# S5 parameters moved to the first feed-forward stage, and a prologue that builds its operand from PSUM, in a three-mixer decoder trunk

## The chip, the cores and the metric

The kernel runs on one core of one Trainium2 chip. The metric is device time of one execution, in microseconds (us); lower is better. Engines are named as the profile names them: PE is TensorE (PEld its weight loads), DVE is VectorE, ACT is ScalarE, POOL is GpSimd, and SP is SyncE, which issues most DMAs here.

## What is computed

A two-layer decoder trunk on 512 tokens of width 1024, all in float32. Each layer adds half a SwiGLU, a mixer (Mamba-2 SSD in layer 0, S5 in layer 1), and half a second SwiGLU; a final normalisation ends it.

```python
def rmsnorm(x, g):
    return x * lax.rsqrt(jnp.mean(x * x, axis=-1, keepdims=True) + NORM_EPS) * g

def swiglu(h, w_in, w_out):
    gate, up = jnp.split(h @ w_in, 2, axis=-1)
    return (jax.nn.silu(gate) * up) @ w_out

for i in range(DEPTH):                       # 2 layers
    x = x + 0.5 * swiglu(rmsnorm(x, ffn1_norm[i]), ffn1_w_in[i], ffn1_w_out[i])
    h = rmsnorm(x, mix_norm[i])
    x = x + (ssd_mixer(h, ...) if i == 0 else s5_mixer(h, ...))
    x = x + 0.5 * swiglu(rmsnorm(x, ffn2_norm[i]), ffn2_w_in[i], ffn2_w_out[i])
return rmsnorm(x, final_norm)
```

The S5 mixer needs operators that depend only on parameters (64 groups of 64 complex states: `lam`, `log_step`, B, C and a skip term `d`). The kernel builds them beside the matmuls of earlier stages and keeps them in DRAM as `d_H`, `d_P` and the phase tables `d_t`.

## The kernel before

Activations are kept transposed, `xT[d]`: eight tiles of 128 channels x 512 tokens. Every projection is split exactly into a high and a low part: `split_w` casts a weight tile `wst` (128 x 1024, 512 KB) on ACT to `whi` and subtracts on DVE to get `wlo`; `proj` then does 24 matmuls per tile (8 blocks x hi·H, hi·L, lo·H). `wst` has four buffers, `whi` and `wlo` three each, and the accumulators `mm` four PSUM banks. So the load of tile n waits until tile n-4 is split, and the cast of tile n waits until PE is done with tile n-3. Below, tile 0, 1, 2, ... are the weight tiles of a feed-forward stage in order: gate and up of f=0, gate and up of f=1, and so on.

Stages run in the order f1_0, ssd, f2_0, f1_1, s5, f2_1. A stage can start its matmuls before the token norm is known, since 1/rms (`rbc`) is applied when the accumulators are read (`gt`, `up`). Four tiles fit into the four banks; the fifth needs `gt` of the first, and so needs `rbc`: squares are summed by `compact_sum` on PE, a Newton iteration of small DVE operations gives `nw_y`, PE broadcasts it (`bcast_rows`), and ACT copies it to `rbc`.

`ffn` calls one closure of its list `fill` after each f and each output tile. Closures of `s5_setup` are handed to f1_0 (part 0: parameters of lambda, powers, tables) and to f2_0 (part 1: it loads back the powers PR, PI, ER, EI, loads B and C in eight pieces with `load_bc`, fills the zero half of `d_P` with `load_d`, and builds the operators with `ops` and `ops_pe`). The order on each engine's queue is set by the build's list scheduler, which also moves instructions of closures ahead of or behind those of the stage; each engine then runs its queue strictly in order. In the prologue x arrives in four DMAs of 512 KB, is transposed on PE in 32 blocks, copied to `xT` on DVE, and made into the operands `hH` and `hL` from `xT`.

Of the kernel before, what the change touches and what calls it, by code (L numbers as in the profile page):

```python
# [1113 lines left out]
```

## Time and profile before

| | |
|---|---|
| median of 3 runs | 2125.33 us (2125.13 to 2127.54) |
| span of the profiled execution | 2124.6 us |
| PE busy | 2055.0 us, 97% of the span |
| DVE, ACT, POOL busy | 1256.6, 793.7, 44.9 us |
| bytes by DMA | 228.50 MB |

The span is the time from the first to the last instruction of one execution; no other time of that execution is recorded, and it lies 0.7 us below the median of the runs. PE carries almost the whole span, so what matters is where PE stands still and at which clock it runs. "Idle" in a row is the time an engine's queue waited just before an instruction, and what is named behind the arrow is what released it.

### The profile page before, as it was taken

How to read it: one execution, taken by the hardware profiler on the slowest of the kernel's cores; microseconds unless marked ns; L12 is line 12 of the kernel's file. 1: busy time of each engine (PE TensorE's matmuls, PEld its weight loads, DVE VectorE, ACT ScalarE, POOL GpSimd, SP SyncE). 2: the span in 40 equal slices, each digit the busy share in tenths (PEclk: the TensorE clock that was granted, in tenths of full speed). 3: DMA queues.
4: the chain of work that ended last, by engine and by line, in shares of the span. 5: the costliest groups of instructions: out<-in, count | busy, mean ns of one | idle time of the engine just before them, and what ended most of it. 6: DMA issues, size and time to landing. Idle time of an engine off the chain costs nothing.

```text
span 2124.6 us, 27175 instructions
## 1 busy us (share of the span) xinstructions
PE 2055.0 (97%) x10755; PEld 1691.2 (80%) x10755; DVE 1256.6 (59%) x2171; ACT 793.7 (37%) x1146; POOL 44.9 (2%) x116
## 2 busy tenths in 40 slices
PE   6999999999999999699999999999996999999997
PEld 5888888888888887587788888888885788888886
DVE  6887445678875787477844454344457654434444
ACT  4223223566753664243422333232254433222222
POOL 1000000000000001000000000000001000000000
PEclk9999999999999999899999999999998999999999
DMA  5344333322223214756533363333357233332331
GB/s 153 110 130 138 91 99 83 99 74 76 70 72 91 77 41 117 123 148 174 154 95 100 94 201 92 99 96 99 95 159 244 83 100 89 99 100 81 108 92 58
DMA packets 408672, 228.50 MB, mean 108 GB/s; under 512 B 45656, under 2 KB 397072, under 8 KB 408544
## 3 DMA queue, kind: packets, MB, share of 16 engines
q1 hardware_dynamic: 383120, 200.24, 33.1%
q0 software_dynamic: 4272, 13.66, 2.8%
q10 hardware_dynamic: 21152, 12.86, 2.1%
q8 instruction: 84, 1.38, 0.3%
q14 instruction: 44, 0.36, 0.1%
HBM read 204.64 MB, written 22.09 MB: 107 GB/s over the span
## 4 chain that ended last, share of the span: by engine, by line
PE 93%; DVE 3%; DMA 2%; ACT 1%; issue 1%; SPq 0%; POOL 0%; ACTq 0%; DVEq 0%
PE mm L203 29%; PE mm L205 29%; PE mm L204 29%; DMA p_B<-in_s_b_re_dram 1%; PE aux L464 1%; PE aux L414 0%; DVE z L919 0%; PE aux L457 0%; DMA wst<-in_ffn_w_in_dram 0%; PE aux L434 0%; DMA p_lrow<-in_s_lam_re_dram 0%; PE aux L135 0%; PE aux L204 0%; PE aux L205 0%; PE aux L203 0%
## 5 line engine op out<-in xcount | busy, mean ns | idle before, releaser
L194 ACT CAST whi<-wst 128x1024 fp32r<-128x1024 f32 (+2 forms) x357 | 361.1, 1013 | 953.6 <-PE mm L204 676.2
L203 PE MATMUL mm<-hH,whi 128*128 128x512 f32 x1800 | 706.4, 393 | 1.2 <-DVE gt L225 1.2
L205 PE MATMUL mm<-hH,wlo 128*128 128x512 f32 x1800 | 703.5, 391 | 0.0
L204 PE MATMUL mm<-hL,whi 128*128 128x512 f32 x1800 | 703.0, 391 | 0.0
L196 DVE TENSOR_TENSOR wlo<-wst,whi 128x1024 fp32r<-128x1024 f32 (+2 forms) x357 | 418.8, 1174 | 107.9 <-ACT whi L194 104.1
L203 PEld LDWEIGHTS mm<-hH,whi 128*128 128x128 f32 x1800 | 339.2, 189 | 73.1 <-issue 2.0
L205 PEld LDWEIGHTS mm<-hH,wlo 128*128 128x128 f32 x1800 | 338.8, 188 | 71.3 <-issue 0.4
L204 PEld LDWEIGHTS mm<-hL,whi 128*128 128x128 f32 x1800 | 339.1, 188 | 69.8
L204 PE MATMUL mm<-al,whi 128*128 128x512 f32 x704 | 275.8, 392 | 0.0
L205 PE MATMUL mm<-ah,wlo 128*128 128x512 f32 x704 | 275.3, 391 | 0.0
L203 PE MATMUL mm<-ah,whi 128*128 128x512 f32 x704 | 274.9, 391 | 0.0
L228 DVE TENSOR_TENSOR up<-mm,rbc 128x512 f32<-128x512 f32 x88 | 60.7, 690 | 222.2 <-PE mm L205 222.1
L240 DVE SCALAR_TENSOR_TENSOR xT<-mm,xT 128x512 f32<-128x512 f32 x96 | 66.1, 689 | 197.6 <-PE mm L205 197.6
L204 PEld LDWEIGHTS mm<-al,whi 128*128 128x128 f32 x704 | 132.1, 188 | 28.7 <-issue 0.2
L205 PEld LDWEIGHTS mm<-ah,wlo 128*128 128x128 f32 x704 | 132.1, 188 | 28.6 <-issue 0.2
L203 PEld LDWEIGHTS mm<-ah,whi 128*128 128x128 f32 x704 | 132.1, 188 | 28.3
L225 DVE TENSOR_TENSOR gt<-mm,rbc 128x512 f32<-128x512 f32 x88 | 60.7, 690 | 154.8 <-PE mm L205 149.4
L231 ACT CAST ah<-up 128x512 fp32r<-128x512 f32 x88 | 54.8, 623 | 66.3 <-DVE up L229 66.2
L340 DVE SCALAR_TENSOR_TENSOR cv<-raw,cols,cv 128x512 f32<-128x512 f32 x96 | 70.9, 745 | 0.7
L229 DVE TENSOR_TENSOR up<-up,gt 128x512 f32<-128x512 f32 x88 | 60.7, 690 | 7.8 <-ACT gt L226 0.7
L226 ACT ACTIVATE gt<-gt 128x512 f32<-128x512 f32 x88 | 55.1, 627 | 17.0 <-DMA d_P<-p_ks 13.2
L233 DVE TENSOR_TENSOR al<-up,ah 128x512 fp32r<-128x512 f32 x88 | 60.1, 684 | 1.4 <-ACT ah L231 1.4
(333 smaller groups left out, 1726.0 us busy)
## 6 DMA issues: line engine op xcount, KB each, us to landing
wst<-in_ffn_w_in_dram SPq DMA_DIRECT2D x176, 512.0 KB, 3.9
wst<-in_ffn_w_out_dram SPq DMA_DIRECT2D x64, 448.0 KB, 3.7
wst<-in_ssd_in_proj_dram SPq DMA_DIRECT2D x48, 512.0 KB, 4.0
wst<-in_ffn_w_out_dram SPq DMA_DIRECT2D x32, 512.0 KB, 4.2
opP<-d_P SPq DMA_DIRECT2D x16, 512.0 KB, 5.0
wst<-in_s_glu_w_dram POOLq DMA_DIRECT2D x12, 512.0 KB, 5.2
d_t<-p_cs POOLq DMA_DIRECT2D x8, 512.0 KB, 3.0
wst<-in_ssd_out_proj_dram SPq DMA_DIRECT2D x8, 512.0 KB, 4.1
```

The lines of the kernel that those rows point to most:

```text
L194: S.copy(hi, st)
L196: V.tensor_tensor(lo, st, hi.bitcast(F32), op=OP.subtract)
L203: PE.matmul(ps, hi[:, k], H[k], start=first and k == 0, stop=False)
L204: PE.matmul(ps, hi[:, k], L[k], start=False, stop=False)
L205: PE.matmul(ps, lo[:, k], H[k], start=False, stop=last and k == n - 1)
L225: V.tensor_tensor(gt, pg, pr.rbc, op=OP.mult)
L226: S.activation(gt, gt, AF.Silu)
L228: V.tensor_tensor(up, pu, pr.rbc, op=OP.mult)
L229: V.tensor_tensor(up, up, gt, op=OP.mult)
L233: V.tensor_tensor(al, up, ah.bitcast(F32), op=OP.subtract)
L240: V.scalar_tensor_tensor(xT[d], po, 0.5, xT[d], op0=OP.mult, op1=OP.add)
L340: V.scalar_tensor_tensor(cv, raw[:, 1 + j:T + 1 + j], col("cw", j * 32 + ct), cv, op0=OP.mult, op1=OP.add)
```

## The change

- B (`load_b`), C (`load_c`), the skip term and the zeros of `d_P` (`zeros`) are loaded or written in f1_0 instead of f2_0. C comes in three DMAs of 256 KB instead of 24 of 32 KB and is transposed there (`c_cols`); B comes in 16 DMAs instead of 32; the second stack of B is made from the first by a copy in SBUF (`swap_b`), and its sign goes into EI.
- The restacked B, B swapped and C are saved to DRAM and loaded back whole in f2_0 (`restore`).
- The zeros are issued from SP instead of POOL.
- The parameter pool of f1_0 no longer lies in the memory of the prologue's x. `tc.keep_in_program_order` (in `paced`, `expf` and others) forbids the scheduler to move that one instruction.
- x comes over SP's and ACT's queues; the first two weight tiles are fetched between its pieces; `hH` and `hL` are made from PSUM, and ACT and DVE run the prologue in written order. Squares come after all operands. The small masks and `cols` of other stages come later.

```diff
+    def paced(dst, src):
+        tc.keep_in_program_order(nc.sync.dma_start(dst, src))
...
-    for j in range(4):
+    def x_in(j, eng):
         js = slice(j * 256, j * 256 + 256)
-        nc.sync.dma_start(xt4[:, :, js], x[0].rearrange("(t p) d -> p t d", p=128)[:, :, js])
+        tc.keep_in_program_order(eng.dma_start(xt4[:, :, js], x[0].rearrange("(t p) d -> p t d", p=128)[:, :, js]))
+    x_in(0, nc.sync)
+    x_in(1, nc.scalar)
...
+    x_in(3, nc.scalar)
...
-            V.tensor_scalar(a, src, -87.0, 88.0, op0=OP.max, op1=OP.min)
+            tc.keep_in_program_order(V.tensor_scalar(a, src, -87.0, 88.0, op0=OP.max, op1=OP.min))
...
+        def load_b(i):
+            gs = slice(i * 8, i * 8 + 8)
+            for h, src in enumerate((s5_b_re, s5_b_im)):
+                paced(st["B1"][h * 64:h * 64 + 64, gs], src[0, gs].rearrange("g p c -> p g c"))
+        def swap_b():
+            for h in range(2):
+                paced(st["B2"][h * 64:h * 64 + 64], st["B1"][64 - h * 64:128 - h * 64])
+        def load_c():
+            st["crow"] = pp.tile([128, 8, 3, 64], F32, name="p_crow", bufs=1)
+            for j, src in enumerate((s5_c_re, s5_c_im, s5_c_re)):
+                paced(st["crow"][:, :, j], src[0].rearrange("(i a) c p -> (a c) i p", a=8))
...
+        def zeros():
             ov = d_P.rearrange("(c q) g m -> q c g m", q=8)
             for q in range(1, 8):
-                G.dma_start(ov[q, :, :, 128:128 + 16 * q], zz[:, None, 0:16 * q].to_broadcast([16, 64, 16 * q]))
+                paced(ov[q, :, :, 128:128 + 16 * q], zz[:, None, 0:16 * q].to_broadcast([16, 64, 16 * q]))
+        def c_cols(i):
+            p = aux_ps()
+            for k in range(2):
+                for j in range(2):
+                    PE.transpose(p[:, j * 256 + k * 128:j * 256 + k * 128 + 128],
+                                 st["crow"][:, 2 * i + k, j:j + 2].rearrange("g a b -> g (a b)"), ident)
+            S.copy(st["C"][:, :, 16 * i:16 * i + 16].rearrange("p a g c -> p a (g c)"),
+                   p.rearrange("p (a n) -> p a n", a=2))
...
+            V.tensor_scalar(EI.rearrange("p a b -> p (a b)"), EI.rearrange("p a b -> p (a b)"), st["sg"][:, 0:1], -1.0,
+                            op0=OP.mult, op1=OP.mult)
...
-            if i % 2 == 0:
-                load_bc(i // 2)
...
-        keep = ("PR", "PI", "ER", "EI")
+        keep = ("ER", "EI", "B1", "B2", "PR", "PI", "C")
         if part == 0:
+            first_loads()
             gen = lam()
-            return [load] + [lambda: next(gen)] * 6 + [save] + [lambda i=i: tables(i) for i in range(8)]
-        return [restore] + [f for i in range(8) for f in (
+            one = lambda: next(gen)
+            return ([both(load_c, masks), zeros, rows] + [one] * 6 + [lambda: save(("PR", "PI", "ER", "EI"))]
+                    + [both(lambda i=i: tables(i), lambda i=i: load_b(i)) for i in range(8)]
+                    + [lambda i=i: c_cols(i) for i in range(4)]
+                    + [lambda: save(("B1",)), swap_b, lambda: save(("C",)), lambda: None, lambda: save(("B2",))])
+        return [lambda: restore(keep[:2]), lambda: restore(keep[2:4]), lambda: restore(keep[4:6]), lambda: restore(keep[6:]),
+                lambda: None, lambda: None] + [f for i in range(8) for f in (
...
-    for d in range(KD):
-        p = aux_ps()
-        for t in range(4):
-            PE.transpose(p[:, t * 128:(t + 1) * 128], xt4[:, t, d * 128:(d + 1) * 128], ident)
-        V.tensor_copy(xT[d], p)
-        prep.take(d)
+    for j in range(2):
+        w0 = ffn1_w_in[0][:, j * FF:j * FF + 128]
+        st_, ins = fetch_w(w0, KD)
+        tc.keep_in_program_order(ins)
+        first.append(st_)
+        if j == 0:
+            x_in(2, nc.sync)
+    with tc.manual_schedule(engines={mybir.EngineType.Activation, mybir.EngineType.DVE}):
+        cols_of(3)
+        for d in range(KD):
+            p = (aux_ps, mm_ps)[d % 4 // 2]()
+            for t in range(4):
+                PE.transpose(p[:, t * 128:(t + 1) * 128], xt4[:, t, d * 128:(d + 1) * 128], ident)
+            g = col(prep.gain[0], prep.gain[1] + d)
+            S.activation(prep.H[d], p, AF.Copy, scale=g)
+            V.scalar_tensor_tensor(prep.L[d], p, g, prep.H[d].bitcast(F32), op0=OP.mult, op1=OP.subtract)
+            if d % 2:
+                S.copy(xT[d], p)
+            else:
+                V.tensor_copy(xT[d], p)
+            if d in (0, 4):
+                ready.append(split_w(first[d // 4], KD))
+        for d in range(KD):
+            prep.square(d)
```

What the engines then have in their queues differs at three places that the prediction uses. Rows of before carry before's line numbers, those of the change its own (L189 became L204, L203 to L205 became L222 to L224, L144 became L160, L594 and L614 became L53).

The first place is SP at the start of the program. Before, it holds x and then the weights of f1_0:

```order
L79 DMA xt_99<-in_x_dram 128x4x256 x4
L189 DMA wst<-in_ffn_w_in_dram 128x8x128 x16
L189 DMA wst<-in_ffn_w_out_dram 128x8x128 x8
L189 DMA wst<-in_ffn_w_in_dram 128x8x128 x14
L189 DMA wst<-in_ffn_w_out_dram 128x7x128 x8
```

Behind x there are only weights. In the change, the same queue from its start to C (`p_crow`); `p_zz` is the tile of zeros:

```order
L85 DMA xt_97<-in_x_dram 128x4x256
L204 DMA wst<-in_ffn_w_in_dram 128x8x128
L85 DMA xt_97<-in_x_dram 128x4x256
L204 DMA wst<-in_ffn_w_in_dram 128x8x128 x4
L53 DMA d_P<-p_zz 16x64x16
L53 DMA d_P<-p_zz 16x64x32
...
L53 DMA d_P<-p_zz 16x64x112
L204 DMA wst<-in_ffn_w_in_dram 128x8x128 x5
L53 DMA p_crow<-in_s_c_re_dram 128x8x64
L53 DMA p_crow<-in_s_c_im_dram 128x8x64
L53 DMA p_crow<-in_s_c_re_dram 128x8x64
```

Seven writes of zeros now stand between weight tiles 4 and 5, and C stands behind tile 9.

The second place is PE in f1_0, where four tiles are done and the norm is broadcast. Before:

```order
L204 MATMUL mm<-hL,whi 128x512
L205 MATMUL mm<-hH,wlo 128x512
L144 MATMUL aux<-ident,nw_y 128x128 x4
L573 MATMUL aux<-ident,p_lrow 128x64 x2
L203 MATMUL mm<-hH,whi 128x512
```

In the change:

```order
L223 MATMUL mm<-hL,whi 128x512
L224 MATMUL mm<-hH,wlo 128x512
L160 MATMUL aux<-ident,nw_y 128x128 x4
L623 MATMUL aux<-ident,p_lrow 128x64 x2
L624 MATMUL aux<-ident,p_drow 16x64
L644 MATMUL aux<-ident,p_crow 128x128 x16
L222 MATMUL mm<-hH,whi 128x512
```

The 16 transposes of C now stand between the broadcast and the first matmul of tile 4. They stood in f2_0 before, two at a time.

The third place is the start of f2_0. DVE before, from the last operand of the stage (`hL`) to the first reading of an accumulator (`gt`), with the Newton rows cut:

```order
L172 SCALAR_TENSOR_TENSOR hL<-xT_95,cols_108,hH 128x512
L543 TENSOR_TENSOR p_Ht<-p_ER,p_B_7594 128x512
L590 TENSOR_SCALAR p_B_7597<-p_B_7597 64x128
L543 TENSOR_TENSOR p_t_7593<-p_EI,p_B_7597 128x512
L543 TENSOR_TENSOR p_Ht<-p_Ht,p_t_7593 128x512
L119 TENSOR_SCALAR nw_v<-aux 128x4
...
L196 TENSOR_TENSOR wlo<-wst,whi 128x1024
L590 TENSOR_SCALAR p_B_7828<-p_B_7828 64x128
L608 COPY p_dT<-aux 16x64
L225 TENSOR_TENSOR gt<-mm,rbc 128x512
```

In the change:

```order
L188 SCALAR_TENSOR_TENSOR hL<-xT_90,cols_104,hH 128x512
L561 TENSOR_TENSOR p_Ht<-p_ER,p_B_7645 128x512
L561 TENSOR_TENSOR p_t_8016<-p_EI,p_B_7647 128x512
L561 TENSOR_TENSOR p_Ht<-p_Ht,p_t_8016 128x512
L135 TENSOR_SCALAR nw_v<-aux 128x4
...
L215 TENSOR_TENSOR wlo<-wst,whi 128x1024
L561 TENSOR_TENSOR p_G_8020<-p_PR,p_C 128x576
L561 TENSOR_TENSOR p_t_8016<-p_PI,p_C 128x576
L245 TENSOR_TENSOR gt<-mm,rbc 128x512
```

The product with B still stands ahead of the Newton iteration, and two products with C now stand ahead of `gt`. SP in the change, at the same place (the first five weight tiles of f2_0, then what is loaded back):

```order
L204 DMA wst<-in_ffn_w_in_dram 128x8x128 x5
L53 DMA p_ER<-d_ER 128x512
L53 DMA p_EI<-d_EI 128x512
L53 DMA p_B_7645<-d_B_2165 128x1024
L53 DMA p_B_7647<-d_B_2288 128x1024
L204 DMA wst<-in_ffn_w_in_dram 128x8x128
L53 DMA p_PR<-d_PR 128x576
L53 DMA p_PI<-d_PI 128x576
L204 DMA wst<-in_ffn_w_in_dram 128x8x128 x2
L53 DMA p_C<-d_C 128x2048
```

C comes last, behind weight tiles 6 and 7, and tile 7 can only be loaded when tile 3 is split.

## Rows read from the trace of the kernel before

**Rows 1.** The page: PE's share of the span, and the span in 40 slices of 53 us (each digit the busy share of PE in tenths).
```profile
PE 2055.0 (97%) x10755; PEld 1691.2 (80%) x10755; DVE 1256.6 (59%) x2171; ACT 793.7 (37%) x1146; POOL 44.9 (2%) x116
PE   6999999999999999699999999999996999999997
```

**Rows 2.** Waits of PE over the whole span: the waiting line, what it waited for, us in total, times, longest.
```profile
PE aux L144 <- DVE nw_y L126: 19.8, 3, 17.3
PE aux L89 <- POOL ident masks.py:199: 8.9, 1, 8.9
```

**Rows 3.** Timeline of SP's DMA queue, then PE, then DVE at the start of f2_0: start, duration, instruction, idle before it and its releaser.
```profile
842.51 0.34 SPq L822 DMA_DIRECT2D p_PR<-d_PR  x1
...
850.40 0.40 PE L205 MATMUL mm<-hH,wlo 128*128 128x512 f32 x1
858.40 0.39 PE L204 MATMUL mm<-hL,whi 128*128 128x512 f32 x1
876.10 1.09 PE L144 MATMUL aux<-ident,nw_y 128*128 128x128 f32 x4 [17.31 <-DVE nw_y L126]
877.91 0.63 PE L203 MATMUL mm<-hH,whi 128*128 128x512 f32 x1
878.34 0.63 PE L204 MATMUL mm<-hL,whi 128*128 128x512 f32 x1
...
868.91 0.69 DVE L543 TENSOR_TENSOR p_Ht<-p_ER,p_B 128x512 f32<-128x512 f32 x1 [22.69 <-DMA p_B<-in_s_b_im_dram]
872.53 0.15 DVE L119 TENSOR_SCALAR nw_v<-aux 128x4 f32<-128x4 f32 x1
873.67 1.22 DVE L196 TENSOR_TENSOR wlo<-wst,whi 128x1024 fp32r<-128x1024 f32 x1
875.87 1.23 DVE L196 TENSOR_TENSOR wlo<-wst,whi 128x1024 fp32r<-128x1024 f32 x1
```

**Rows 4.** The DMA view of 850 to 858 us: packets, MB and the time that packets took, as a share of 16 engines (q0 is POOL's queue, q1 SP's).
```profile
q0 software_dynamic: 175, 0.59, 92.1%
q1 hardware_dynamic: 706, 0.04, 6.0%
```

**Rows 5.** The DMA view of 842 to 850 us, the issue of zeros: size in KB and the time to landing of the last of them.
```profile
d_P<-p_zz POOLq DMA_DIRECT2D x1, 448.0 KB, 22.2
```

**Rows 6.** All issues that load B: time to landing.
```profile
DMA to landing us min/median/max: 2.3/3.0/24.1
```

**Rows 7.** Stretches around the wait in f2_0 and one of f1_0: length, busy time of the engines, then PEclk (the granted clock of TensorE as a share of 2.4 GHz), DMA share and GB/s.
```profile
858.40:862.00 3.60, 0.38 (x2) 0.00 (x0) 0.00 (x0) 0.00 (x0) 0.00 (x0) 1.00 1.00 85
862.00:864.00 2.00, 0.00 (x0) 0.00 (x0) 0.00 (x0) 0.00 (x0) 0.00 (x0) 0.87 1.01 89
876.00:880.40 4.40, 4.30 (x12) 3.28 (x13) 3.69 (x7) 1.96 (x3) 0.00 (x0) 0.50 0.76 208
80.00:120.00 40.00, 40.00 (x178) 33.06 (x177) 38.05 (x140) 11.51 (x15) 2.39 (x4) 1.00 0.40 120
```

**Rows 8.** Timeline of f1_0 where the norm is broadcast: POOL, DVE and PE.
```profile
38.32 0.58 POOL L566 DMA_DIRECT2D p_step<-in_s_log_step_dram  x1 [29.45 <-PE aux L89]
...
43.86 0.20 DVE L548 TENSOR_SCALAR p_ea<-p_step 128x64 f32<-128x64 f32 x1 [2.88 <-DMA p_step<-in_s_log_step_dram]
...
45.25 0.62 PE L144 MATMUL aux<-ident,nw_y 128*128 128x128 f32 x4 [1.56 <-DVE nw_y L126]
47.43 0.48 PE L573 MATMUL aux<-ident,p_lrow 64*128 64x64 f32 x2 [1.56 <-DMA p_lrow<-in_s_lam_re_dram]
49.09 0.80 PE L203 MATMUL mm<-hH,whi 128*128 128x512 f32 x1 [1.18 <-DVE gt L225]
54.37 0.47 PE L203 MATMUL mm<-hH,whi 128*128 128x512 f32 x1
```

**Rows 9.** Timeline of the prologue: ACT, DVE, PE.
```profile
13.39 1.04 ACT L194 CAST whi<-wst 128x1024 fp32r<-128x1024 f32 x1 [0.80 <-DMA wst<-in_ffn_w_in_dram]
...
15.75 0.68 DVE L1041 COPY xT<-aux 128x512 f32<-128x512 f32 x1
18.81 0.73 DVE L172 SCALAR_TENSOR_TENSOR hL<-xT,cols,hH 128x512 fp32r<-128x512 f32 x1
...
20.25 0.55 PE L204 MATMUL mm<-hL,whi 128*128 128x512 f32 x1
```

**Rows 10.** Stretches of the prologue, columns as in Rows 7; the last number is the GB/s of all DMAs.
```profile
2.70:9.00 6.30, 0.07 (x1) 0.07 (x1) 0.00 (x0) 0.00 (x0) 4.28 (x10) 1.00 1.07 346
3.00:4.00 1.00, 0.00 (x0) 0.00 (x0) 0.00 (x0) 0.00 (x0) 1.00 (x3) 1.00 1.07 376
9.00:16.00 7.00, 4.08 (x17) 3.24 (x17) 3.37 (x8) 2.92 (x3) 0.00 (x0) 1.00 1.16 287
```

**Rows 11.** The DMA view of 916 to 917 us and of 917 to 918 us, ACT's queue alone (q10), which there carries writes of 64 to 512 bytes from 16 partitions to `d_P`: packets, MB, share of 16 engines.
```profile
q10 hardware_dynamic: 513, 0.18, 77.6%
...
q10 hardware_dynamic: 538, 0.07, 45.8%
```

**Rows 12.** The transposes of C before: min, median and max ns of one.
```profile
L597 PEld LDWEIGHTS aux<-ident,p_crow x16: 138/142/143, 885.1 to 1037.9; 128*128 128x128 f32 x16
```

**Rows 13.** The page: DMA issues of two kinds, KB each, median us from issue to landing.
```profile
wst<-in_ffn_w_in_dram SPq DMA_DIRECT2D x176, 512.0 KB, 3.9
...
opP<-d_P SPq DMA_DIRECT2D x16, 512.0 KB, 5.0
```

More of the change, by code (lines that the diff above doesn't have):

```diff
@@ L90, in cols_of @@
         V.tensor_copy(cols[i], p[:, :n])
-    nc.scalar.dma_start(vrow[3], rows_ap(ffn1_norm, 0, 16))
-    cols_of(3)
+    tc.keep_in_program_order(nc.scalar.dma_start(vrow[3], rows_ap(ffn1_norm, 0, 16)))
+    x_in(3, nc.scalar)
     r = 0
@@ L106, in trunk_kernel, with late_cols @@
                     bass.AP(tensor=src.tensor, offset=src.offset, ap=[[32, 1], [0, 4], [1, 32]]))
+    def late_cols():
+        V.tensor_copy(vrow[2][0:16].rearrange("a (h p) -> a h p", p=64), sdr[:, :, None].to_broadcast([16, 2, 64]))
+        for i in range(3):
+            cols_of(i)
     def col(nm, j=0, n=1):
@@ L110, in col, with both @@
         return cols[i][:, r0 + j:r0 + j + n]
+    def both(*fs):
+        return lambda: [f() for f in fs]
     def newton_rsqrt(ps4, n, scale):
@@ L205, in proj, with ffn @@
             PE.matmul(ps, lo[:, k], H[k], start=False, stop=last and k == n - 1)
-    def ffn(pr, w_in, w_out, nxt, fill=()):
-        fill = list(fill)
+    def ffn(pr, w_in, w_out, nxt, fill=(), ready=()):
+        fill, ready = list(fill), list(ready)
         def pop():
@@ L535, in s5_setup @@
             s5["t"] = [dram.tile([128, 2, 8, 64], F32, name=f"d_t{i}") for i in range(8)]
+            s5["dT"] = const.tile([16, 64], F32, name="p_dT")
         d_H, d_P, d_t = s5["H"], s5["P"], s5["t"]
@@ L562, in expf, with first_loads @@
             tt(o, t, r_, OP.mult)
-        def load():
+        def first_loads():
             st["step"] = sm("step")
-            G.dma_start(st["step"], bass.AP(tensor=s5_log_step.tensor, offset=s5_log_step.offset, ap=[[0, 128], [1, 64]]))
-            lrow = pp.tile([64, 2, 2, 64], F32, name="p_lrow", bufs=1)
+            G.dma_start(st["step"], bass.AP(tensor=s5_log_step.tensor, offset=s5_log_step.offset,
+                                               ap=[[0, 128], [1, 64]]))
+            st["lrow"] = lrow = pp.tile([64, 2, 2, 64], F32, name="p_lrow", bufs=1)
             for i, src in enumerate((s5_lam_re, s5_lam_im)):
@@ L783, in ops_pe @@
             gs = slice(i * 4, i * 4 + 4)
-            h4 = slice(i % 2 * 4, i % 2 * 4 + 4)
             Ht, G9 = st["w"]
@@ L1036, in trunk_kernel @@
     prep = prep_for(stages[0])
-    for d in range(KD):
-        p = aux_ps()
-        for t in range(4):
-            PE.transpose(p[:, t * 128:(t + 1) * 128], xt4[:, t, d * 128:(d + 1) * 128], ident)
-        V.tensor_copy(xT[d], p)
-        prep.take(d)
-    for i in range(3):
-        cols_of(i)
+    pre0 = s5_setup(pre, 0)
+    first = []
+    for j in range(2):
[5 more added lines that the diff above has]
+            x_in(2, nc.sync)
+    ready = []
+    with tc.manual_schedule(engines={mybir.EngineType.Activation, mybir.EngineType.DVE}):
[5 more added lines that the diff above has]
+            g = col(prep.gain[0], prep.gain[1] + d)
+            prep.H[d] = hpool.tile([128, T], F32R, name="hH")
+            S.activation(prep.H[d], p, AF.Copy, scale=g)
+            prep.L[d] = hpool.tile([128, T], F32R, name="hL")
+            V.scalar_tensor_tensor(prep.L[d], p, g, prep.H[d].bitcast(F32), op0=OP.mult, op1=OP.subtract)
+            if d % 2:
+                S.copy(xT[d], p)
+            else:
+                V.tensor_copy(xT[d], p)
[3 more added lines that the diff above has]
+            prep.square(d)
+    late_cols()
     xin_es.close()
@@ L1064, in trunk_kernel @@
             wi, wo = (ffn1_w_in, ffn1_w_out) if s[:2] == "f1" else (ffn2_w_in, ffn2_w_out)
-            if s in s5_pre:
-                with tc.tile_pool(name="pre", bufs=2) as pp:
-                    ffn(pr, wi[L], wo[L], nxt, fill=s5_setup(pp, s5_pre.index(s)))
+            if s in s5_pre[:1]:
+                ffn(pr, wi[L], wo[L], nxt, fill=pre0, ready=ready)
+                pre_es.close()
+            elif s in s5_pre:
+                with tc.tile_pool(name="pre1", bufs=2) as pp:
+                    ffn(pr, wi[L], wo[L], nxt, fill=s5_setup(pp, 1))
             elif stages[i + 1] == "s5":
```

96 lines of the change are left out of this document (43 added, 53 removed).

## The prediction

> **What bounds the kernel now.** The page comes first: PE is busy for 2055.0 of 2124.6 us, and its 40 slices show the rest in a few holes, of which the change touches two, the first slice and the eighteenth [rows 1]. The list of PE's waits names them: the broadcast of the norm waits for `nw_y` (19.8 us in three times, 17.3 in one), and the first transposes for the identity (8.9) [rows 2].
>
> Then the timelines. In f2_0 PE starts its last matmul before the norm at 858.40 and the broadcast at 876.10, after 17.31 us idle. DVE is the cause: its next instruction is `p_Ht`, a product of S5 parameters, which stood idle 22.69 us for B, and Newton is queued behind it [rows 3]. B's loads have 32 KB each and land in 3.0 us as a rule, but in 24.1 here [rows 6]. In that stretch POOL's queue, which writes zeros, has 92.1% of the DMA engines' time and SP's 6.0% [rows 4]; the last zeros land 22.2 us after issue [rows 5]. So B is late because the zeros run beside it. The clock adds a little: granted 1.00 until 862, then falling, and 0.50 (1.2 GHz) until 880.4 [rows 7]. A matmul starts every 0.43 us there, against 0.229 before (35 steps from 850.40 to 858.40) [rows 3].
>
> In f1_0 POOL issued the load of `p_step` only after 29.45 us, since its memory was x's; DVE met `p_ea`, which needs it, in the middle of Newton and stood 2.88 us. PE waited 1.56, 1.56 (for `p_lrow`) and 1.18 us (for `gt`) and then ran 12 matmuls from 49.09 to 54.37, 5.3 us instead of 12 x 0.229 = 2.75. Tile 4 therefore begins as if at 49.09 + 2.5 = 51.6 at full clock [rows 8].
>
> **The prologue and f1_0 up to tile 4.** x, three weights in advance and `vrow` come at the rate of [rows 10]: 346 GB/s from 2.7 to 9 us, 2.18 MB, then 287 GB/s. Before, the first transpose waits for the identity until 8.9 [rows 2]; now POOL makes it after three DMA issues and x's first half megabytes are there at some 5.5 (1.05 MB at 376 GB/s from 2.7, the start of the transfers by the window of [rows 10]). Counting 2 us for the two blocks PE does first, PE reaches block 0 at about 8 and ACT has its first `hH` at 9.1. From there DVE is the chain: the differences for blocks 0 to 2, two copies to `xT` and one `wlo`, 3 x 0.73 + 2 x 0.68 + 1.22 = 4.8 [rows 3, 9]; I add 0.9 for what it waits between them, one more `hL` with its signal. At 14.8 the first accumulator bank is free and the stream of matmuls starts; before it started at 20.25 [rows 9]. Its 96 matmuls take 22.0 us. PE now meets blocks 6 and 7 late (their `hL` at about 22), but works on two or three tiles by then; I add 1.5 us of waits (bounds 0 and 4). With the matmuls of the sums and `cols` (1.3, an estimate of three groups at the 0.4 to 0.5 of such small ones [rows 3, 8]) the broadcast stands at 39.6, and with `p_lrow` and the skip term PE is at C's transposes at 40.9.
>
> There it waits for C. C's load stands behind weight tile 9, which needs tile 5 split, which needs PE done with tile 2: 14.8 + 1.5 + 72 x 0.229 = 32.8, plus cast 1.04, subtraction 1.22 and 0.2 between, 35.3. A weight lands 3.9 us after issue [rows 13], so 39.2. C is 3072 packets of 256 bytes. No row has such a DMA; its price is bounded by packets of 130 bytes at 13.7 ns and of 350 at 24.2 (0.458 x 16 us / 538 and 0.776 x 16 / 513) [rows 11], so 2.6 to 4.6 us over 16 engines; in between by size, 19.6 ns, 3.8 us. C lands at 43.0. The wait is 2.1 us (bounds 0 and 5), the transposes take 16 x 0.155 = 2.5 (a fourth of the 0.62 of four at full clock [rows 8]), and tile 4 starts at 45.5. Against 51.6 that is **-6.1 us**. I let the clock stay up: PE's idle time here is half of that before.
>
> The zeros are the risk of this part. They are 7 x 1024 pieces of 64 to 448 bytes, 1.84 MB, and now stand in SP's queue between tiles 4 and 5. x and five weights are 4.72 MB, through by 9 + 2.54/0.287 = 17.8 [rows 10]. At 19.6 ns a packet the zeros take 8.8 us, tile 5 lands at 17.8 + 8.8 + 1.8 (0.52 MB at 287) = 28.4, and is wanted at 32.8. So they cost nothing until they take 13.2 us; the cover is the four tiles that PE can do without a norm.
>
> **Two queues for x.** One queue already moved 346 GB/s up to 9 us and 376 at best [rows 10], so I take nothing for bandwidth; the gain above is from the identity, and from `hH` and `hL` made without waiting for `xT`. [...]
>
> **f2_0.** B comes back in whole rows, and no zeros run beside it. ER, EI, B1 and B2 are 1.57 MB, issued from 842.5 as the first of the powers was [rows 3]; at 287 GB/s [rows 10] with 2 us latency (an estimate: 3.9 for a weight [rows 13] less 1.8 for its bytes) they are there at 850.0. DVE does its three products by 851.4 and Newton by 854.8 (3.4 us, with one subtraction `wlo` inside: 872.53 to 875.87 before [rows 3]). PE wants `nw_y` at 858.6, so this wait ends: 17.3 us.
>
> What is late next is C. It is 1.05 MB behind tile 7, and tile 7 is issued when tile 3 is split, 2.4 us into Newton, 853.8 [rows 3]. In the queue stand tiles 5 and 6, the other powers and tile 7, 2.16 MB from 850.0, 857.5; C takes 3.7 more, 861.2. DVE then does two products and `gt` (3 x 0.69 by the product `p_Ht` of [rows 3], 2.1 us) and tile 4 starts at 863.4; PE was ready at 859.5, so 3.9 us of the 17.3 come back. Bounds: 0, if C lands by 857; 7 us, if C needs 10 us from its issue at 854.2 (twice the 5.0 of half its size [rows 13]), and 2.2 more if the clock falls, as it did 4 to 5 us after PE stopped [rows 7]. I take 3.9 and no fall, being nearer to the rate of the weights, which C's long rows should reach. Before, tile 4 started at 877.91 and lost 6 x 0.20 = 1.2 to the clock: 877.9 + 1.2 - 863.4 = **-15.7 us**. C's transposes leave the full stream of f2_0: 16 x 0.142 = **-2.3** [rows 12]; they are already counted in f1_0.
>
> **Costs taken as nothing.** B's 8192 packets now come beside f1_0's output tiles. At 10.9 ns (0.06 x 8 us x 16 / 706 [rows 4]) they are 5.6 us of transfers, in eight pieces, under weights fetched four tiles ahead. DVE's extra scaling of EI is one 0.69 us instruction against eight sign changes removed; where DVE was fullest, 38.05 of 40 us, PE never stopped [rows 7]. Without that cover each microsecond would be PE's. Saving B, its swap and C adds 2 MB to POOL's queue.
>
> **Sum.** -6.1 - 15.7 - 2.3 = -24.1. The span was 2124.6, so 2100.5; the median lies 0.7 above that span, so **2101.2 us**.
>
> **Rivals.** (a) The zeros take as long as they did from POOL: 0.59 MB at 8 x 0.921 us is 80 GB/s [rows 4], 23 us. Tile 5 then lands at 42.6, Newton waits for its split on DVE, and C (behind four weights, 7.2, and its own 3.8) lands at 53.9; with transposes at half clock (4.4) tile 4 starts at 58.3, 12.8 later than forecast: 2114. For it: the destination and the pieces are the same. Against: [rows 11], ACT's writes from 16 partitions at 180 GB/s. [...]
> (b) The slower end of the same mechanism: every piece of zeros, now a packet of its own, costs what POOL's packets of 3.4 KB cost, 0.921 x 8 x 16 / 175 = 0.67 us [rows 4]. That is 300 us, weights starve, and the time is near 2390. It turns into a loss from 79 ns a packet (35 us). Against it stand 14 to 24 ns [rows 11].
> (c) C replaces B as the wait of f2_0, with the bounds above: 7 us idle and 2.2 of clock, 2106.5.
> (d) No change: the zeros near 35 us, 2125.
>
> **Chances.** Forecast 0.68 (own range 2097 to 2105: each wait of C from 0 to 4 us more), (a) 0.12, (b) 0.03, (c) 0.12, (d) 0.05. The range 2095 to 2114 holds the forecast, (c) and half of (a). 0.2% (4.3 us) is about what a measurement tells from no change: faster 0.92, same 0.05, slower 0.03.
>
> **What would show it.** In the changed trace: matmuls streaming from about 15 us; PE's wait at the transposes of C near 41, a few us; DVE's wait before `p_Ht` near 848 a few us instead of 22.7, and one before `p_G` at about 856 to 861 that PE follows with some 4 us. If weight tile 5 lands after 33 us, or the zeros' issues on SP stretch far beyond 10 us, (a) or (b) holds. I am wrong if PE waits in f1_0 at places the list above doesn't have.

## The result, and the profile after

The change takes the median from 2126.19 us (2125.13 to 2127.54, 4 runs) to 2108.16 us (2107.50 to 2109.67, 4 runs), a ratio of 0.9918 with a 95% interval of 0.9904 to 0.9932. That is 18.0 us faster, where 24.1 were forecast; the time lies within the stated range. The profiled spans differ by 18.8 us (2124.6 and 2105.8).

The page of after, which answers to [rows 1]: PE's share, the span in 40 slices, and the granted clock in the same slices.

```profile
PE 2054.7 (98%) x10755; PEld 1691.9 (80%) x10755; DVE 1255.9 (60%) x2157; ACT 793.4 (38%) x1146; POOL 41.0 (2%) x114
...
PE   6999999999999999999999999999996999999997
...
PEclk8999999999999999999999999999997999999999
```

PE does the same work, and the hole in the eighteenth slice is gone. The first slice is no better than before, and its clock is down to 8 tenths from 9. The waits of PE in after, to be read beside [rows 2]:

```profile
PE aux L160 <- DVE nw_y L142: 6.1, 2, 5.1
...
PE mm L222 <- DVE xT L1102: 3.2, 1, 3.2
...
PE aux L644 <- DMA p_crow<-in_s_c_im_dram: 2.9, 1, 2.9
```

The 17.3 us wait for `nw_y` has become one of 5.1, and it stands elsewhere. The stages are told apart by comparing the same instruction in both timelines of DVE. Here are the last `gt` of f1_0, the first of f1_1 and the first of f2_1, before:

```profile
348.22 0.69 DVE L225 TENSOR_TENSOR gt<-mm,rbc 128x512 f32<-128x512 f32 x1 [2.35 <-PE mm L205]
...
1253.67 0.69 DVE L225 TENSOR_TENSOR gt<-mm,rbc 128x512 f32<-128x512 f32 x1 [3.97 <-ACT rbc L183]
...
1767.87 0.69 DVE L225 TENSOR_TENSOR gt<-mm,rbc 128x512 f32<-128x512 f32 x1 [1.02 <-ACT rbc L183]
```

and the same three in after:

```profile
352.68 0.69 DVE L245 TENSOR_TENSOR gt<-mm,rbc 128x512 f32<-128x512 f32 x1 [2.35 <-PE mm L224]
...
1236.49 0.69 DVE L245 TENSOR_TENSOR gt<-mm,rbc 128x512 f32<-128x512 f32 x1 [3.96 <-ACT rbc L199]
...
1749.02 0.69 DVE L245 TENSOR_TENSOR gt<-mm,rbc 128x512 f32<-128x512 f32 x1 [1.02 <-ACT rbc L199]
```

After is 4.5 us late at the end of f1_0, 17.2 ahead at the start of f1_1 and 18.9 ahead at the start of f2_1. So f1_0 lost 4.5 where the forecast had a gain of 6.1. The ssd stage and f2_0 together gained 21.6, nearly all of it in f2_0, which was to gain 18.0. The last 1.7 came in f1_1 and s5, which the change doesn't touch; in the other kernels below this stretch moved by up to 3.6 us (e4 against after) without any edit there, so I read nothing into it.

What happened in f1_0 stands in the timeline of after (SP, ACT, DVE, PE):

```profile
13.56 15.63 SPq L53 DMA_DIRECT2D d_P<-p_zz  x7
29.29 15.13 SPq L204 DMA_DIRECT2D wst<-in_ffn_w_in_dram  x5
44.47 0.83 SPq L53 DMA_DIRECT2D p_crow<-in_s_c_re_dram  x1
...
41.72 1.04 ACT L213 CAST whi<-wst 128x1024 fp32r<-128x1024 f32 x1 [8.89 <-PE mm L224]
...
42.80 1.23 DVE L215 TENSOR_TENSOR wlo<-wst,whi 128x1024 fp32r<-128x1024 f32 x1 [8.97 <-ACT whi L213]
43.94 0.15 DVE L135 TENSOR_SCALAR nw_v<-aux 128x4 f32<-128x4 f32 x1
...
46.81 1.09 PE L160 MATMUL aux<-ident,nw_y 128*128 128x128 f32 x4 [5.13 <-DVE nw_y L142]
51.33 3.89 PE L644 MATMUL aux<-ident,p_crow 128*128 128x128 f32 x16 [2.92 <-DMA p_crow<-in_s_c_im_dram]
54.87 0.78 PE L222 MATMUL mm<-hH,whi 128*128 128x512 f32 x1
...
57.58 0.41 PE L222 MATMUL mm<-hH,whi 128*128 128x512 f32 x1
```

The zeros hold SP's queue from 13.56 to 29.19. Tile 5 is issued behind them and is cast only at 41.72. The trace puts this wait down to PE, but PE was done with tile 2 by then: with quick zeros (e2) the same cast starts at 34.42. So it was the load. DVE's queue has the subtraction of tile 5 ahead of Newton, so `nw_y` is late, and PE waits 5.1 us with its four tiles done. C stands behind tile 9 in SP's queue, is issued at 44.47, and PE waits again. The transposes and the first 6 matmuls of tile 4 run at half clock (granted 0.50 from 51.33 to 57.58; the traces give the clock as a share of full speed, and no run shows it in GHz). The rate of the zeros is in the DMA view of 20 to 25 us (packets, MB, share of 16 engines):

```profile
q1 hardware_dynamic: 1818, 0.41, 66.8%
```

0.41 MB in 5 us is 83 GB/s, about the 80 of POOL's queue in [rows 4], and a third of the engines' time is idle meanwhile.

In f2_0 the timeline of PE and DVE shows the other side:

```profile
862.74 0.60 PE L160 MATMUL aux<-ident,nw_y 128*128 128x128 f32 x4
863.09 0.48 PE L224 MATMUL mm<-hH,wlo 128*128 128x512 f32 x1
...
869.55 0.39 PE L222 MATMUL mm<-hH,whi 128*128 128x512 f32 x1
...
852.27 0.69 DVE L561 TENSOR_TENSOR p_Ht<-p_ER,p_B 128x512 f32<-128x512 f32 x1 [1.89 <-DMA p_B<-d_B]
...
865.72 0.76 DVE L561 TENSOR_TENSOR p_G<-p_PR,p_C 128x576 f32<-128x576 f32 x1 [4.49 <-DMA p_C<-d_C]
...
867.06 0.68 DVE L245 TENSOR_TENSOR gt<-mm,rbc 128x512 f32<-128x512 f32 x1
```

`p_Ht` waits 1.89 us for B instead of the 22.69 of [rows 3], and PE has no wait here. PE reaches the broadcast at 862.74, some 4.1 us later than before (858.6), so C, for which `p_G` waits until 865.7, came about when it was forecast (861.2 on the time axis of before). It costs nothing all the same. In PE's queue the broadcast stands inside tile 2: 20 of its 24 matmuls are ahead of it, then come 4 more and the 24 of tile 3, and only the 29th after it, at 869.55, begins tile 4 and needs `gt`. `gt` ended at 867.7. The kernel before has the same 28 matmuls there; these are the second and the 29th behind its wait of 17.31 us (the first, at 877.32, is missing from [rows 3]):

```profile
877.91 0.63 PE L203 MATMUL mm<-hH,whi 128*128 128x512 f32 x1
...
885.47 0.48 PE L203 MATMUL mm<-hH,whi 128*128 128x512 f32 x1
```

So tile 4 started at 885.47 before, and not at 877.91.

### The profile page after: what moved, and what is told of

It is laid out like the page before. It is cut to its first block, busy times and chain, and to the rows that moved or that the text cites. A ratio compares the mean times of both kernels' runs of the same rounds, so it can differ in the third digit from the quotient of the medians.

```text
span 2105.8 us, 27114 instructions
## 1 busy us (share of the span) xinstructions
PE 2054.7 (98%) x10755; PEld 1691.9 (80%) x10755; DVE 1255.9 (60%) x2157; ACT 793.4 (38%) x1146; POOL 41.0 (2%) x114
## 4 chain that ended last, share of the span: by engine, by line
PE 95%; DVE 3%; ACT 1%; DMA 1%; issue 1%; ACTq 0%; SPq 0%; DVEq 0%
PE mm L222 30%; PE mm L223 29%; PE mm L224 29%; PE aux L484 1%; PE aux L434 0%; PE aux L477 0%; PE aux L454 0%; PE aux L151 0%; PE aux L978 0%; DVE z L960 0%; PE aux L223 0%; PE aux L222 0%; PE aux L224 0%; PE aux L404 0%; PE aux L455 0%
## 5 line engine op out<-in xcount | busy, mean ns | idle before, releaser
L222 PE MATMUL mm<-hH,whi 128*128 128x512 f32 x1800 | 704.7, 392 | 3.2 <-DVE xT L1102 3.2
L224 PE MATMUL mm<-hH,wlo 128*128 128x512 f32 x1800 | 702.2, 390 | 0.0
L222 PEld LDWEIGHTS mm<-hH,whi 128*128 128x128 f32 x1800 | 338.6, 188 | 75.0 <-ACT hH L1096 3.4
L224 PEld LDWEIGHTS mm<-hH,wlo 128*128 128x128 f32 x1800 | 338.6, 188 | 71.0 <-issue 0.6
L224 PE MATMUL mm<-ah,wlo 128*128 128x512 f32 x704 | 275.3, 392 | 0.0
L222 PE MATMUL mm<-ah,whi 128*128 128x512 f32 x704 | 274.7, 392 | 0.0
L222 PEld LDWEIGHTS mm<-ah,whi 128*128 128x128 f32 x704 | 132.1, 188 | 28.9 <-issue 0.6
L224 PEld LDWEIGHTS mm<-ah,wlo 128*128 128x128 f32 x704 | 132.1, 188 | 28.6 <-issue 0.2
```

What stands on the lines that cost most here:

```text
L222: PE.matmul(ps, hi[:, k], H[k], start=first and k == 0, stop=False)
L224: PE.matmul(ps, lo[:, k], H[k], start=False, stop=last and k == n - 1)
```

## The experiments

Each edit is against the changed kernel where nothing else is said. `Z` stands for `zz[:, None, 0:16 * q].to_broadcast([16, 64, 16 * q])`, the source of one write of zeros. Where the source needs more partitions or columns, the tile `zz` is made larger; that line is left out.

**e1: zeros spread over f1_0.**

```diff
-        def zeros():
+        def zeros(q):
...
-    [both(load_c, masks), zeros, rows] + [one] * 6 + [lambda: save(("PR", "PI", "ER", "EI"))]
+    [both(load_c, masks), lambda: None, rows] + [both(one, lambda q=q: zeros(q)) for q in range(1, 7)]
+        + [both(lambda: save(("PR", "PI", "ER", "EI")), lambda: zeros(7))]
```

> The change with the seven writes of zeros spread over f1_0 (one behind each of seven steps of the parameters) instead of all between weight tiles 4 and 5. Theory (the zeros hold up tile 5 on SP's queue, and with it Newton and C): tile 5 lands by about 25 us, the 5.1 us wait for nw_y is gone, tile 4 starts at 46 to 48 instead of 54.9, and the time is 2099 to 2101 us. Rival (tile 5 was not what PE waited for, the norm chain itself is late): the wait for nw_y stays above 3 us and the time stays within 2 us of 2108.

Measured: 2101.72 us (2099.53 to 2103.02), ratio to before 0.9886 (0.9870 to 0.9903). PE in that timeline:

```profile
41.59 0.60 PE L160 MATMUL aux<-ident,nw_y 128*128 128x128 f32 x4
44.63 0.63 PE L645 MATMUL aux<-ident,p_crow 128*128 128x128 f32 x4 [2.12 <-DMA p_crow<-in_s_c_im_dram]
```

The wait for `nw_y` is gone and the rival falls. The time and the start of tile 4 (45.02) miss their expected ranges by under 1 us. Only 4 of the 16 transposes of C stand ahead of tile 4 here, the others come later; but the last `gt` of f1_0 is at 342.92 instead of 352.68, so the gain is not only moved. All the zeros at once between tiles 4 and 5 made the loss of f1_0.

**e2: zeros from 64 partitions.** This is also the base of e6 and e7.

```diff
-    paced(ov[q, :, :, 128:128 + 16 * q], Z)
+    paced(ov[q, :, :, 128:128 + 16 * q].rearrange("c g m -> g c m"),
+          zz[:, None, 0:16 * q].to_broadcast([64, 16, 16 * q]))
```

> The change with the zeros read from 64 partitions (the group index) instead of 16; the pieces, their bytes, their number and the place on SP are as they were. Theory S1 (the source sets the rate: 16 partitions, each giving the same few bytes again and again): the writes of zeros run at well over 150 GB/s instead of 83 to 100, are done in 7 to 12 us instead of 17, tile 5 lands by 33, and the time is 2099 to 2103. Theory S2 (the destination's short pieces set the rate): still 80 to 100 GB/s, tile 5 at about 41, the time within 2 us of 2108.

Measured: 2099.46 us (2098.31 to 2101.25), ratio 0.9876 (0.9862 to 0.9891). The DMA view of 20 to 25 us, and PE's first matmul of tile 4:

```profile
q1 hardware_dynamic: 3557, 0.98, 96.4%
```

```profile
46.21 0.48 PE L222 MATMUL mm<-hH,whi 128*128 128x512 f32 x1
```

The same pieces now run at 197 GB/s, the engines are full, and a packet costs 0.964 x 5 x 16 / 3557 = 21.7 ns. Tile 4 starts at 46.21, where the forecast had 45.5. Theory S1 holds in its first half (the source, not the pieces); which property of the source, the next runs ask.

**e3: every piece 512 bytes.**

```diff
-    paced(ov[q, :, :, 128:128 + 16 * q], Z)
+    paced(ov[q, :, :, 128:256], zz[:, None, :].to_broadcast([16, 64, 128]))
```

> The change with every piece of zeros 512 bytes long, the whole second half of a row of d_P (what lies in the half is overwritten later, as before): the same 7168 pieces, 3.67 MB instead of 1.84. Theory by bytes (83 to 100 GB/s whatever the piece): 37 to 44 us for the zeros, tile 5 lands near 60, the time about 2125 to 2130. Theory by pieces (14 to 33 ns each on 16 engines): 6 to 17 us, time near 2108 or below. Theory of short pieces (under 512 bytes a piece costs more than its bytes): at 512 bytes about 287 GB/s, 13 us, tile 5 by 35, the time near 2102.

Measured: 2127.25 us (one run). PE waits 23.89 us for `nw_y`. The DMA view of 20 to 25 us:

```profile
q1 hardware_dynamic: 961, 0.48, 78.1%
```

0.48 MB is 97 GB/s with pieces of 512 bytes, 83 with pieces half that size. The theory by bytes holds. Neither the number of pieces nor a threshold at 512 bytes sets this rate.

**e4: zeros from POOL's queue, in f1_0.**

```diff
-    paced(ov[q, :, :, 128:128 + 16 * q], Z)
+    tc.keep_in_program_order(G.dma_start(ov[q, :, :, 128:128 + 16 * q], Z))
```

> The change with the zeros issued by POOL again (in f1_0, at its place in the order of the program) instead of SP. Theory Q (what costs is that the weights stand behind the zeros in one queue): tile 5 lands early, the wait for nw_y goes, 2099 to 2102. Theory D (what costs is the time that the zeros hold the 16 DMA engines, as in f2_0 before): the weights land late beside them, up to 20 us from issue, the wait for nw_y or one in the first four tiles is 5 us or more, 2105 to 2115.

Measured: 2108.30 us (2 runs), ratio 0.9917 (0.9897 to 0.9937), the same as the change. ACT in the timeline, and POOL's queue from 18 to 30 us:

```profile
39.99 1.04 ACT L213 CAST whi<-wst 128x1024 fp32r<-128x1024 f32 x1 [7.65 <-DMA wst<-in_ffn_w_in_dram]
```

```profile
q0 software_dynamic: 395, 1.30, 101.4%
```

Tile 5 is nearly as late beside the zeros as behind them (two weights issued in that window took 19.0 us to land, where 3.8 is the median in the change). Theory D holds: POOL's packets fill the 16 engines (101.4%), though they move no more than 1.30 MB in 12 us, 108 GB/s.

**e5: the kernel before, with the zeros at the end of f2_0's operators.**

```diff
+            st["zz"] = zz
...
+        def zeros():
+            V.tensor_tensor(st["zz"], st["ks"][:, 0, 0:112], st["ks"][:, 0, 0:112], op=OP.subtract)
...
-    lambda i=i: (ops_pe(2 * i), ops(2 * i + 1)))] + [lambda: ops_pe(15)]
+    lambda i=i: (ops_pe(2 * i), ops(2 * i + 1)))] + [lambda: (ops_pe(15), zeros())]
```

> The kernel before with one thing changed: the zeros of d_P are written after the last step of the operators in f2_0 (their source is made there from ks minus ks, so that they can't start sooner), and not while B is being loaded. Theory (B was late in f2_0 because the zeros ran beside it): B lands about 3 us after issue, DVE's wait of 22.7 us before p_Ht falls under 5, PE's wait for nw_y in f2_0 (17.3 us) and the half clock behind it (1.2) go, and the time is 2106 to 2109 us, most of what f2_0 gives in the change. Rival (B's own 64-byte pieces are slow): PE still waits 10 us or more there and the time is above 2115.

Measured: 2121.97 us (2120.06 to 2124.86, 8 runs), ratio 0.9978 (0.9968 to 0.9988). The time misses the range that goes with the theory; the trace bears the theory out all the same. DVE at the start of f2_0, POOL at the zeros, DVE and PE behind them:

```profile
849.82 0.69 DVE L543 TENSOR_TENSOR p_Ht<-p_ER,p_B 128x512 f32<-128x512 f32 x1 [2.95 <-DMA p_B<-in_s_b_im_dram]
...
1032.93 5.38 POOL L620 DMA_DIRECT2D d_P<-p_zz  x7 [188.57 <-DVE p_zz L616]
...
1042.90 0.69 DVE L225 TENSOR_TENSOR gt<-mm,rbc 128x512 f32<-128x512 f32 x1 [1.56 <-PE mm L205]
...
1065.45 0.80 PE L203 MATMUL mm<-hH,whi 128*128 128x512 f32 x1 [11.71 <-ACT whi L194]
```

The wait for B falls from 22.69 to 2.95 us, PE no longer waits for `nw_y` in f2_0, and the `gt` of 1042.90 comes 18.9 us before its fellow in the kernel before (1061.76). That is the gain the theory put at 18.5. Then the zeros start, weights are late, PE waits 11.7 us, and 13.9 of the 18.9 are given back. So B was late because of the zeros, and the zeros cost about as much in the next place.

**e6: x on one queue (on e2).**

```diff
-    x_in(1, nc.scalar)
+    x_in(1, nc.sync)
...
-    x_in(3, nc.scalar)
+    x_in(3, nc.sync)
```

> The kernel of the run with 64 source partitions, with x's four pieces all on SP's queue (three of them ahead of the first weight) instead of two on SP's and two on ACT's. Theory (a second queue brings no bandwidth, and one queue moves as much): the stream of matmuls starts at 16.1 to 17.1 us as with two queues (16.6), and the time is 2098 to 2101. Rival (two queues bring x in sooner): the last piece lands 2 us or more later, the stream starts after 18.5, and the time is 2101 to 2104.

Measured: 2101.56 us (2100.70 to 2103.63), ratio 0.9883 (0.9867 to 0.9900); e2's interval covers it. The time lies in the rival's range, but the rival's late stream isn't there. The stream starts neither late nor at the same time, but sooner. PE, and the stretch behind it (columns as in [rows 7]):

```profile
15.27 0.77 PE L222 MATMUL mm<-hH,whi 128*128 128x512 f32 x1 [1.87 <-DVE xT L1102]
```

```profile
15.20:21.00 5.80, 5.73 (x14) 4.51 (x15) 4.68 (x7) 4.43 (x7) 0.00 (x0) 0.50 1.16 224
```

It starts 1.3 us before e2's 16.61 and runs at half clock until 21, and the broadcast comes at 41.37 against 41.42. Up to there the second queue is worth nothing that can be measured. Behind it, e6's trace has half clock after the wait at C, where e2's has full clock, and the last `gt` of f1_0 comes at 344.26 against 342.78. Whether that belongs to the queue isn't shown.

**e7: C ahead of the zeros (on e2).**

```diff
-    [both(load_c, masks), zeros, rows]
+    [masks, both(load_c, zeros), rows]
```

> The kernel with 64 source partitions, and C loaded in the same step as the zeros, so that on SP it stands behind weight tile 3 and ahead of tile 4 and the zeros instead of behind tile 9. Theory (the 2.0 us that PE waits at the transposes of C come from C's place in the queue alone): the wait is 0, tile 4 starts at about 44.2 instead of 46.2, and the time is 2097 to 2098. Rival (0.79 MB more ahead of tiles 4 and 5 delay Newton): a wait for nw_y of 1 to 3 us appears and the time is 2099 or more.

Measured: 2098.36 us (2097.11 to 2099.38), ratio 0.9866 (0.9851 to 0.9880).

```profile
41.19 0.62 PE L160 MATMUL aux<-ident,nw_y 128*128 128x128 f32 x4 [0.84 <-DVE nw_y L142]
...
42.06 1.99 PE L644 MATMUL aux<-ident,p_crow 128*128 128x128 f32 x16
43.81 0.48 PE L222 MATMUL mm<-hH,whi 128*128 128x512 f32 x1
```

No wait at C, and tile 4 starts 2.4 us before e2's. Only about 1.2 us of that is C's place: the wait of 2.03 us is gone, and the rival's wait for `nw_y` has come in its stead, but with 0.84 us and not 1 to 3. The other 1.2 us come from the stream of matmuls, which is granted full clock from its start here (1.00 from 16.5 to 21) and ends that much sooner. This beats both kernels: its interval lies wholly under that of the change. Against e2 the times alone don't tell.

**e8: 16 partitions, but never the same address twice in a row.**

```diff
-    paced(ov[q, :, :, 128:128 + 16 * q], Z)
+    paced(ov[q, :, :, 128:128 + 16 * q],
+          bass.AP(tensor=zz.tensor, offset=zz.offset, ap=[list(zz.ap[0]), [4, 64], [1, 16 * q]]))
```

> The change with the zeros still read from 16 partitions, the destination and its order as they are, but each of the 64 pieces of a partition read 16 bytes further on than the one before instead of all from the same address. Theory R (the same bytes read again and again are what is slow): well over 150 GB/s, tile 5 lands by 33, 2099 to 2103 us. Theory P (16 partitions, or the order of the rows in the destination that goes with them, set the rate): 80 to 100 GB/s as before, 2106 to 2110 us.

Measured: 2109.38 us (one run). From 20 to 25 us:

```profile
q1 hardware_dynamic: 1797, 0.39, 58.4%
```

77 GB/s: repeating an address isn't what is slow.

**e9: 16 partitions, in e2's order of destination rows.**

```diff
-    paced(ov[q, :, :, 128:128 + 16 * q], Z)
+    for j in range(4):
+        gs = slice(16 * j, 16 * j + 16)
+        paced(ov[q, :, gs, 128:128 + 16 * q].rearrange("c g m -> g c m"),
+              zz[:, None, 0:16 * q].to_broadcast([16, 16, 16 * q]))
```

> The change with the zeros written in the order of the 64-partition run (a group's 16 rows, then the next group), but from 16 source partitions: four DMAs for each q, 28 in all, at the same place on SP, the same pieces and bytes. Theory P (the number of source partitions sets the rate): 80 to 100 GB/s in the stretch of the zeros, tile 5 at about 41, 2106 to 2110 us. Theory O (the order of the rows in the destination sets it): 130 GB/s or more, at the larger pieces 180, tile 5 lands by 35, 2099 to 2103.

Measured: 2109.22 us (one run). From 30 to 35 us, with the larger pieces:

```profile
q1 hardware_dynamic: 1330, 0.50, 76.4%
```

100 GB/s, against 98 in the change at the same time: the order of the destination isn't it either.

**e10: C loaded back twice in f2_0.**

```diff
     paced(st[nm], v)
+    if nm == "C":
+        paced(st[nm], v)
```

> The change with C loaded back twice in f2_0, the second load into the same tile, so that DVE's two products and gt come later by a shift S that the trace shows (5 to 9 us). Theory (the 28 matmuls that stand between the broadcast and tile 4 in f2_0 cover C; gt ended 1.6 us before PE wanted tile 4): PE waits S minus 1.6 us (0.7 either way) at tile 4 and the time is 2112 to 2116. Rival (tile 4 stands right behind the broadcast, as the prediction had it, and other work filled the time): PE waits the whole of S, or shows no new wait at all.

Measured: 2108.74 us (one run), no new wait. The delay that was to be tested didn't come about, since the scheduler put the products with C behind `gt`:

```profile
863.66 0.69 DVE L245 TENSOR_TENSOR gt<-mm,rbc 128x512 f32<-128x512 f32 x1 [3.46 <-ACT rbc L199]
...
869.48 0.76 DVE L561 TENSOR_TENSOR p_G<-p_PR,p_C 128x576 f32<-128x576 f32 x1 [2.02 <-DMA p_C<-d_C]
```

So how much delay the 28 matmuls cover isn't tested; that `gt` is in time by 1.8 us (867.7 and 869.55) rests on the trace of after. But e10 moves `gt` the other way: it starts 1.3 us behind the broadcast (862.40) and not 4.3 (862.74 and 867.06), and from the broadcast to the first `gt` of f1_1 both kernels take the same time (373.8 us, to 1236.20 and 1236.49). An earlier `gt` gains nothing, as it must be if tile 4 doesn't wait for it.

**e11: zeros from 128 partitions**, in two DMAs of 64 for each q.

```diff
-    paced(ov[q, :, :, 128:128 + 16 * q], Z)
+    for h in range(2):
+        paced(ov[q, 8 * h:8 * h + 8, :, 128:128 + 16 * q].rearrange("c g m -> g c m"),
+              zz[64 * h:64 * h + 64, None, 0:16 * q].to_broadcast([64, 8, 16 * q]))
```

> The change with the zeros read from 128 partitions (two DMAs for each q, one from the lower and one from the upper 64), same pieces, bytes and place on SP. Theory (each source partition gives so much; 16 gave 83 to 100 GB/s, 64 gave 185 to 200): if the rate still grows with partitions, over 250 GB/s and done in 7 us; if the price of a packet on a busy engine (19.7 ns with 64 partitions) is the bound by then, 185 to 210 GB/s and no gain over 64 partitions. Tile 5 lands by 30 in both cases and the time is 2097 to 2101.

Measured: 2098.86 us (one run). From 20 to 25 us:

```profile
q1 hardware_dynamic: 3661, 1.00, 93.7%
```

201 GB/s and 20.5 ns a packet, with twice the partitions of e2 and engines nearly as full. With 64 partitions the packets had become the bound.

**e12: 16 partitions, 8 apart.**

```diff
-    paced(ov[q, :, :, 128:128 + 16 * q], Z)
+    paced(ov[q, :, :, 128:128 + 16 * q],
+          bass.AP(tensor=zz.tensor, offset=zz.offset, ap=[[8 * zz.ap[0][0], 16], [0, 64], [1, 16 * q]]))
```

> The change with the zeros read from 16 partitions that lie 8 apart (0, 8, 16 to 120) instead of 0 to 15; destination, order, pieces, bytes and place on SP are as in the change. Theory N (the number of source partitions sets the rate: 16 gave 80 to 105 GB/s, 64 gave 197): 80 to 105 GB/s again, tile 5 at about 41, 2106 to 2110 us. Theory W (where the source partitions lie sets it: 0 to 15 share a few ways out of SBUF, and partitions spread over all 128 have more): 180 to 200 GB/s, tile 5 lands by 33, 2097 to 2101. [...]

Measured: 2100.66 us (one run). From 20 to 25 us:

```profile
q1 hardware_dynamic: 3227, 0.87, 91.8%
```

174 GB/s (a little under the 180 expected) with as few partitions as the change, which has 83 in the same stretch. Theory W holds in what it says of the rate: what counts is where the source partitions lie. The reason that the theory gives for it was supposed, and no run shows it.

## Why the prediction was right, and where its steps failed

The time lies in the stated range because that range held half of rival (a) too. It missed the 2097 to 2105 that the forecast gave itself, and f1_0 went as (a) has it. An error of 10.6 us in f1_0 stands against errors of 3.6 and 1.7 us the other way, so the size of the gain is in part luck.

**What bounds the kernel: right.** The wait for `nw_y` in f2_0 came from B, and B was late because of the zeros beside it (e5: 22.69 to 2.95 us).

**f1_0 up to tile 4: wrong by 10.7 us.** Tile 4 was to start at 45.5; it starts at 54.87 and loses 1.3 more to the clock (6 matmuls in 2.71 us instead of 1.37). The step that failed is the price of the zeros, "at 19.6 ns a packet the zeros take 8.8 us". The price was near for writes that fill the engines (20.5 to 21.7 ns in e11 and e2), but it assumed that the 16 engines are the limit. From partitions 0 to 15 the source is (83 GB/s, against 174 in e12 and 197 in e2), and a packet costs 0.668 x 5 x 16 / 1818 = 29.4 ns of an engine that idles for a third of the time: 1.84 MB at 83 to 100 GB/s are 18 to 22 us, above the 13.2 that the forecast allowed. So f1_0 went the way of rival (a), which had a chance of 0.12 and forecast tile 5 at 42.6 (cast at 41.72) and tile 4 at 58.3 (54.87). The sign that the prediction named for it was there: tile 5 after 33 us, and issues of zeros that stretch over 15.6. The argument against (a), ACT's writes at 180 GB/s [rows 11], was drawn from a burst of 0.3 MB. Why that burst is quicker than 100 GB/s isn't settled by these runs. The 10.7 us are: the stream's end 1.9 later, the wait for `nw_y` with its delay 5.3, C's wait 0.8 more than forecast, its transposes 1.0 more, the clock in tile 4 1.3, the small groups at half clock 0.3; the rest is rounding.

**The start of the stream: 14.8 forecast, 16.52 measured.** Two things were left out. ACT loads a table (1.28 us) ahead of its first `hH`, and PE runs at about half clock behind a wait of 3.2 us for a free bank (granted 1.00 before it, 0.54 behind it):

```profile
8.62 1.28 ACT L1096 ACT_TABLE_LOAD   x1 [8.62 <-DVE cols L99]
```

```profile
16.50:20.24 3.74, 3.72 (x10) 2.93 (x11) 2.62 (x5) 3.18 (x5) 0.00 (x0) 0.54 1.27 206
```

Nine matmuls in 3.72 us instead of 9 x 0.229 = 2.06 are 1.7 us. Against that, the 1.5 us added for blocks 6 and 7 didn't come.

**C's place in f1_0: right in kind.** The wait at `p_crow` is 2.9 us (2.1 forecast), it is 2.0 with quick zeros (e2), and it goes when C is loaded early (e7, for a wait of 0.84 us at `nw_y`). The forecast's chain holds once the zeros are quick: tile 4 at 46.21 in e2.

**Two queues for x, 0: right as far as the stream goes** (the broadcast at 41.37 with one queue in e6, at 41.42 with two in e2).

**f2_0: 3.6 us too small, the ssd stage included.** The step that failed is "tile 4 starts at 863.4; PE was ready at 859.5, so 3.9 us of the 17.3 come back". It took tile 4 to stand right behind the broadcast, as it does in f1_0. In f2_0 28 matmuls lie between, 6.4 us of cover, in both kernels: the row at 877.91, which the prediction took for the start of tile 4 before, is the second of the 28, and tile 4 started at 885.47. That misreading stands on both sides of the difference and drops out, but the 3.9 us of waiting for C were put where those 28 matmuls cover them. With the 3.9 left out, the forecast is 18.0 + 3.9 = 21.9, and 21.6 with the ssd stage is what was measured. Rival (c) was off for the same reason.

**Costs taken as nothing: right.** The lag against before is 4.5 us at the third `gt` of f1_0 (61.9 us) and 4.5 at the last, beside B's small pieces and DVE's extra work.

## What to carry to other kernels

Before a bulk write is moved under something else, find what limits its rate. If its share of the DMA engines is well under 100% while nothing else runs (66.8% here), look at its ends; here the cure was in the source's layout: the same zeros from 64 partitions, or from 16 that lie 8 apart, ran at twice the rate (197 and 174 GB/s, against 83). (On POOL's queue the share read 101.4% at 108 GB/s in e4, so read the GB/s too.) Moved as one lump it only moves the bill: beside B in f2_0, in f1_0 on SP, in f1_0 on POOL and late in f2_0 it cost some 9 to 19 us each time. In seven pieces with other transfers between them (e1) it cost little from the same 16 partitions, too: e1's time is 2.3 us above e2's, and their intervals overlap. And where a wait is said to end at a tile, count the matmuls that stand between the broadcast and that tile in that stage; two stages of one kernel differ by 28.

## What was not expected of the hardware

On SP's queue the zeros ran at 77 to 100 GB/s from the sixteen partitions 0 to 15 (e8, the change, e3, e9), and at 174 from 16 spread over 128 (e12). A wait of PE of about 2 us was followed by full clock in some kernels and by half clock in others. The stretch behind the wait at `p_crow` in e2 (waited 2.03 us), in e6 (2.08 us) and in e12 (1.85 us):

```profile
44.30:47.80 3.50, 3.43 (x23) 3.03 (x24) 2.77 (x5) 2.93 (x6) 0.00 (x0) 1.00 0.54 156
```

```profile
44.30:47.80 3.50, 3.43 (x12) 2.79 (x13) 3.41 (x7) 2.01 (x4) 0.00 (x0) 0.59 0.54 156
```

```profile
44.30:47.80 3.50, 3.46 (x17) 3.26 (x18) 2.92 (x5) 2.46 (x5) 0.00 (x0) 0.59 0.57 157
```

The first was granted 1.00 (as were e1, behind 2.12 us, and e11, behind 1.76, in the same stretch) and the other two 0.59, so a short wait's price in clock can't be read from its length alone here. Each of them is one profiled execution of a different kernel, so whether the kernel or chance makes the difference stays open.
